# Transposing block-diagonal probabilities on VectorE, and output and gate rows of the samples by column groups, in a hybrid attention and DeltaNet decoder step

## The chip, the cores and the metric

The kernel runs on one core of one Trainium2 chip. The metric is the device time of one execution in microseconds.

## The reference

One inference step of a decoder layer with two parallel branches, for a prompt of 512 tokens and for 8 samples of 4 tokens each (32 rows). A conditioning vector `c` per sequence (1 for the prompt, 8 for the samples) gives shift, scale and gate. Branch A is softmax attention over three groups of heads with dilations 1, 4 and 16; branch B a gated DeltaNet. What the change touches is the gate, the attention's probabilities and the last lines, the output projection with its residual and LayerNorm:

```python
def layer_front(x, c, w_cond, b_cond, w_in):
    shift, scale, gate = jnp.split(jax.nn.silu(c) @ w_cond + b_cond, 3, axis=-1)
    h = x * (1 + scale[:, None]) + shift[:, None]
    return gate, split_columns(h @ w_in)
...
def dilated_attend(q, k_slab, v_slab, pos0, dilation, bias_hj):
    ...
    logits = jnp.einsum('bqhd,bqjhd->bqhj', q, k_sel, preferred_element_type=jnp.float32) * (A_HEAD_DIM ** -0.5)
    logits = logits + bias_hj.astype(jnp.float32)
    logits = jnp.where(valid[:, None, :], logits, -jnp.inf)
    m = jnp.max(logits, axis=-1, keepdims=True)
    p = jnp.exp(logits - m)
    s = jnp.sum(p, axis=-1, keepdims=True)
    out = jnp.einsum('bqhj,bqjhd->bqhd', p / s, v_sel.astype(jnp.float32))
...
def layer_back(x, gate, o_a, za, o_b, zb, ga, gb, b_norm_w, w_branch_a, w_branch_b, w_out, ln_g, ln_b):
    ...
    merged = jax.nn.sigmoid(ga) * (ya @ w_branch_a) + jax.nn.sigmoid(gb) * (yb @ w_branch_b)
    r = (ALPHA * x + gate[:, None] * (merged @ w_out)).astype(jnp.float32)
    mu = jnp.mean(r, axis=-1, keepdims=True)
    var = jnp.mean(jnp.square(r - mu), axis=-1, keepdims=True)
    return ((r - mu) * lax.rsqrt(var + LN_EPS)).astype(dtype) * ln_g + ln_b
```

`ALPHA` is 2 to the power 1/4; D_MODEL is 1024. Beside the two outputs `y`, the step returns updated key and value caches and states, which are mostly copied.

## The kernel before

The whole step is one program. Python functions record operations on symbolic tiles (`Recorder.add`), each with a rank; `Recorder.schedule` then places all of them with a list scheduler that has its own table of costs, and `emit` writes them in that order. So nearly all instructions carry one line, L723, and tiles have to be told apart by name. An operation counts as ready when the operations that it needs are done plus a margin, `Recorder.margin`: 0.1 for a compute operation on another engine, 0.5 for a transfer. Within an engine the order is then fixed, and each engine runs its instructions strictly in that order. All transfers are issued on SP's queue, the copies of the caches (`out_kv_s<-in_cache`) among them, which the scheduler puts between the others.

Products with the large weights are done in three products each (high part by high part, low by high, high by low) on `F32R` tiles. These are the stream of column jobs: 544 columns (512 prompt tokens and 32 sample rows) in two halves of 272, tiles `pp<-hhi,hi` and the like. Weights come in as `wt`, ScalarE makes the high part `hi`, VectorE the low part `lo`. PSUM has 2 banks for `pp`, 2 for `pd`, 3 for `pg`, 1 for `pb`. While the stream runs, threads of smaller work are mixed in: attention of the prompt, attention of the samples, DeltaNet.

**Attention of the prompt** (`prompt_attention`) runs over 4 head pairs `j`, 4 query blocks `i` of 128 queries, 2 heads `hh`. `scores` makes a tile `P` of 128 queries by 512 keys: 256 for group 0 (the block before and the own one), 128 for group 1 and 128 for group 2. In group 2 the dilation is 16, keys and queries are sorted by their residue, and `bias_indices` lets a query see only keys with `a == k // 32`, so that outside four 32x32 diagonal blocks all entries are zero after the exponential. TensorE transposes the quarters of `P` (3 of them for `i` = 0, else 4) into a bank `pg`; ScalarE (for `hh` = 0) or VectorE (`hh` = 1) copies them into `PT`, and `PT` is the moving operand of the products with `vrow`.

**Gate rows** (`gate_rows`, rank 1, between the column jobs of branch A): `gate` is `silu(c) @ w_cond + b_cond` for 9 rows (prompt and 8 samples). For each half `n` of 512 columns, 8 products `pd<-wc,cs` in two groups of 4; each of the four writes its own 32 partitions of a bank (`tile_position`), so the sum over the four partition groups is still to be taken. ScalarE copies the bank to `Y`, and two products with constant selections add up the groups and spread the rows: one makes `gp`, the prompt's row on 128 partitions, the other `gs`, the sample rows on 64. VectorE adds them to the bias, which was loaded into `gp` and `gs` beforehand.

**Output rows.** `merge_after` makes high and low parts `mhi`, `mlo` of `merged` and, for the 32 sample rows, a tile `ms` of 64 columns (high and low side by side). `load_out` loads `w_out` in four pieces of 512 KB per half (`wo`, through the 3 buffers of `wraw`) and makes `wo0h`, `wo0l`, `wo1h`, `wo1l`. The last loop goes over `ORDER`, pairs of a half `n` and a token tile `tt` (4 is the samples): 24 products of 512 columns for a token tile; 16 of 64 columns over 512 for the samples. VectorE multiplies by the gate, which frees the bank, adds the scaled input `xr`, takes the statistics, and after the second half normalizes; then `y` is written.

## Time and profile before

| what | us |
|---|---|
| median of three runs | 901.5 (900.58 to 903.18) |
| the profiled execution, its own time | 900.46 |
| its span in the profile | 898.7 |
| TensorE matmuls busy | 877.9 (98%) |
| VectorE busy | 718.9 (80%) |
| ScalarE busy | 428.7 (48%) |
| transfers, mean busy share of the 16 engines | 79% (the main queue) |

The profile shows one execution. Starts are counted from the span's start. A matmul's shown duration is longer than the time for which it keeps TensorE from the next one, since matmuls are pipelined: what one costs is read from the distance of starts. A fp32 product appears as two matmuls, a product of `F32R` tiles as one, a transpose as one.

### The profile page before, as it was taken

What the parts mean: (1) busy time and instruction counts of PE and PEld (TensorE: products, weight loads), DVE (VectorE), ACT (ScalarE), POOL (GpSimd) and SP (SyncE); (2) the same over time, 40 slices, a digit from 0 to 9 for tenths busy, and PEclk for the clock granted to TensorE, in tenths of its full rate; (3) what the DMA queues carried; (4) which work ended last, traced back from release to release, by engine and by line L of the source; (5) the groups of instructions that cost most, each with busy time, mean ns of one, the idle gap of its engine ahead of it and who ended that gap; (6) DMA issues with size and microseconds to landing.
All of it is one profiled execution on the core that took longest, in us unless ns stands there. A gap on an engine that the chain in (4) does not pass through costs nothing.

```text
span 898.7 us, 20349 instructions
## 1 busy us (share of the span) xinstructions
PE 877.9 (98%) x7864; PEld 827.9 (92%) x7864; DVE 718.9 (80%) x1580; ACT 428.7 (48%) x1054; POOL 51.0 (6%) x115
## 2 busy tenths in 40 slices
PE   8999999999999999999999999999999999999996
PEld 7889998999999998997999998999999999998676
DVE  3576657677669999987999997577989989958677
ACT  3474645676445776344666444544432222234321
POOL 0110010001000020000020000011010000000000
PEclk9999999999999999999999999999999999999999
DMA  9867787366787888897788887499799999989842
GB/s 367 317 177 217 219 237 245 141 175 228 229 254 253 246 259 283 260 310 249 265 270 278 245 290 229 135 324 391 229 336 347 348 407 410 356 259 334 305 130 100
DMA packets 104197, 239.39 MB, mean 266 GB/s; under 512 B 31955, under 2 KB 58589, under 8 KB 100389
## 3 DMA queue, kind: packets, MB, share of 16 engines
q1 hardware_dynamic: 103956, 238.08, 78.8%
q8 instruction: 62, 1.02, 0.4%
q14 instruction: 35, 0.28, 0.1%
q10 hardware_dynamic: 144, 0.01, 0.0%
HBM read 221.48 MB, written 104.26 MB: 362 GB/s over the span
## 4 chain that ended last, share of the span: by engine, by line
PE 84%; DMA 5%; DVE 4%; ACT 4%; issue 1%; POOL 1%; SPq 1%; DVEq 0%; POOLq 0%; ACTq 0%
PE pp L723 64%; PE pg L723 10%; PE pd L723 7%; PE pb L723 3%; DMA wt<-in_w_in 1%; DMA xT<-in_xT 1%; DMA wf<-in_w_first 1%; ACT L723 1%; DVE acc L723 1%; DMA wm<-in_w_mod 1%; DVE lo L723 1%; POOL ext L723 1%; ACT QKd L723 1%; SPq L723 1%; ACT hi L723 1%
## 5 line engine op out<-in xcount | busy, mean ns | idle before, releaser
L723 PE MATMUL pp<-hhi,hi 128*128 128x272 f32 x1360 | 399.0, 293 | 3.5 <-ACT ext L723 1.2
L723 PE MATMUL pp<-hlo,hi 128*128 128x272 f32 x1360 | 399.6, 294 | 0.0
L723 PE MATMUL pp<-hhi,lo 128*128 128x272 f32 x1360 | 398.7, 293 | 0.0
L723 PEld LDWEIGHTS pp<-hhi,hi 128*128 128x128 f32 x1360 | 256.5, 189 | 5.7 <-issue 2.4
L723 PEld LDWEIGHTS pp<-hhi,lo 128*128 128x128 f32 x1360 | 256.2, 188 | 2.4 <-issue 1.8
L723 PEld LDWEIGHTS pp<-hlo,hi 128*128 128x128 f32 x1360 | 256.6, 189 | 1.9 <-issue 1.2
L723 ACT ACTIVATE hi<-wt 128x1024 fp32r<-128x1024 f32 (+1 forms) x101 | 103.7, 1027 | 151.5 <-PE pp L723 123.0
L723 DVE TENSOR_TENSOR lo<-wt,hi 128x1024 fp32r<-128x1024 f32 (+1 forms) x101 | 118.7, 1175 | 37.3 <-ACT hi L723 36.5
L723 DVE SCALAR_TENSOR_TENSOR acc<-ext,cw,acc 128x568 f32<-128x568 f32 x72 | 57.1, 800 | 8.0 <-ACT acc L723 7.7
L723 ACT ACTIVATE P<-P,st 128x256 f32<-128x256 f32 (+1 forms) x64 | 31.2, 488 | 29.5 <-DVE st L723 29.2
L723 DVE TENSOR_TENSOR slab<-slab 128x512 f32<-128x512 f32 (+1 forms) x66 | 42.9, 664 | 2.6 <-DMA slab<-qd 2.6
L723 DVE TENSOR_REDUCE slab<-slab 128x8 f32<-128x512 f32 (+2 forms) x66 | 42.8, 658 | 0.2
L723 PE MATMUL pp<-ybl,hi 128*128 128x272 f32 x128 | 37.1, 290 | 0.0
L723 PE MATMUL pp<-ybh,hi 128*128 128x272 f32 x128 | 36.9, 288 | 0.0
L723 PE MATMUL pp<-ybh,lo 128*128 128x272 f32 x128 | 36.8, 288 | 0.0
L723 ACT ACTIVATE zt<-pp 128x272 f32<-128x272 f32 x48 | 18.7, 389 | 37.7 <-PE pp L723 34.4
L723 ACT ACTIVATE q<-pp 64x272 f32<-64x272 f32 (+1 forms) x48 | 26.3, 549 | 18.8 <-PE pp L723 18.2
L723 ACT ACT_TABLE_LOAD x26 | 33.4, 1283 | 1.6 <-PEq L2348 1.2
L723 PE MATMUL pg<-k,q 128*128 128x128 f32 (+1 forms) x192 | 33.6, 308 | 0.0
L723 PEld LDWEIGHTS pg<-k,q 128*128 128x128 f32 x192 | 27.3, 191 | 2.6 <-issue 1.3
L723 DVE CUSTOM_DVE_ANT_0 P<-pg,bias 128x256 f32<-128x256 f32 (+1 forms) x64 | 23.4, 399 | 5.7 <-PE pg L723 5.5
L723 DVE TENSOR_TENSOR tmp<-Ls,Tb 32x15 f32<-32x15 f32 (+7 forms) x120 | 23.1, 193 | 5.2 <-DMA Ls<-dblk 1.7
(399 smaller groups left out, 1601.9 us busy)
## 6 DMA issues: line engine op xcount, KB each, us to landing
out_kv_s<-in_cache SPq DMA_DIRECT2D x144, 512.0 KB
wt<-in_w_in SPq DMA_DIRECT2D x85, 512.0 KB
out_kv_s<-in_cache SPq DMA_DIRECT2D x24, 496.0 KB
wm<-in_w_mod SPq DMA_DIRECT2D x8, 1024.0 KB
slab<-in_ks SPq DMA_DIRECT2D x32, 256.0 KB
slab<-in_vs SPq DMA_DIRECT2D x32, 256.0 KB
kv<-in_ks SPq DMA_DIRECT2D x16, 512.0 KB
kv<-in_vs SPq DMA_DIRECT2D x16, 512.0 KB
```

What stands on the lines that cost most here:

```text
L723: getattr(real[x.engine], x.name)(*map(arg, x.args), **{k: arg(v) for k, v in x.kw.items()})
```

## The change

- **Attention.** TensorE transposes the first three quarters of `P` only. The last one (group 2) is transposed by VectorE, from `P` straight into `PT`, as `STREAM_TRANSPOSE`, which transposes within 32x32 blocks. The copies out of `pg` are narrower by 128 columns.
- **Gate rows.** All 8 products of a half stand in one group. The selection takes 9 columns and runs twice over 256 columns, each on its own column group, so that the 9 rows lie in 4 column blocks (`b4`), where the bias is added. These are written to DRAM (`dg`), and `gp` and `gs` are read back from there; `gs` now has 4 column blocks of 256 on 4 x 32 partitions.
- **Sample rows** (`sample_rows`, at (1, 4); (0, 4) is gone). In fp32, with `ms` of 32 columns as the stationary operand: for each of 8 `k`, four products over 256 columns of `w_out`, each on its own column group. The raw pieces of `w_out` are its moving operands: for the second half those that `load_out` has loaded (the fourth into a buffer of its own), for the first half four loaded again (`wr`). Means over 1024 columns are taken over the four groups by two products with a constant (`QUARTER`).
- **Margins.** `nudge` gives each operation a margin of its own out of a random generator: over all operations 0.35 to 0.65 for transfers and 0.06 to 0.14 for the others, and in 25 stretches of the recording, other values of one of three kinds (a transfer's margin, 0.3 to 0.9; the other margin, 0 to 0.2; TensorE's patience before it changes the tile form).

```diff
--- before.py
+++ after.py
-ORDER = ((0, 4), (0, 0), (0, 1), (0, 2), (1, 0), (1, 4), (1, 1), (1, 2), (0, 3), (1, 3))
+NUDGES = (
+    (0, 9912, 1047), (572, 972, 696727), (6242, 7442, 352100), (4626, 5026, 884219), (8230, 9430, 221759),
...
+ORDER = ((0, 0), (0, 1), (0, 2), (1, 0), (1, 4), (1, 1), (1, 2), (0, 3), (1, 3))
...
+QUARTER = (np.arange(128)[:, None] % 32 == np.arange(128)[None, :] % 32).astype(np.float32) / 4
...
+    def nudge(self):
+        for lo, hi, seed in NUDGES:
+            rng, kind = np.random.default_rng(seed), seed % 3 if lo else 3
+            for op in self.ops[lo:hi]:
+                x = rng.uniform()
+                if kind in (0, 3):
+                    op.load_margin = 0.3 + 0.6 * x if kind == 0 else 0.35 + 0.3 * x
+                if kind in (1, 3):
+                    op.own_margin = 0.2 * x if kind == 1 else 0.06 + 0.08 * rng.uniform()
+                if kind == 2 and op.engine == "pe":
+                    op.hold = self.HOLD * (0.5 + 1.2 * x)
+
     def schedule(self):
         ops = self.ops
         tag, lines = {}, {}
+        self.nudge()
...
-        return 0.1 if p.transfer is None else 0.5
+        return getattr(op, "own_margin", 0.1) if p.transfer is None else getattr(op, "load_margin", 0.5)
...
-                    for c in range(c0_, 4):
+                    for c in range(c0_, 3):
                         pe.transpose(pt[:, 128 * c:128 * c + 128], Ps[hh][:, 128 * c:128 * c + 128], ident)
                     PT = ap.tile([128, 4, 128], F32, name="PT", bufs=2)
                     eng = ve.tensor_copy if hh else (lambda o, x: se.activation(o, x, AF.Copy))
-                    eng(PT[:, c0_:], cols128(pt)[:, c0_:])
+                    eng(PT[:, c0_:3], cols128(pt)[:, c0_:3])
+                    ve.transpose(PT[:, 3], Ps[hh][:, 384:512])
...
-        sp.dma_start(gp, b.to_broadcast([128, D]))
-        sp.dma_start(gs, b.to_broadcast([64, D]))
+        b4 = al.tile([128, 256], F32, name="b4")
+        for q in range(4):
+            sp.dma_start(b4[32 * q:32 * q + 9], b[:, 256 * q:256 * q + 256].to_broadcast([9, 256]))
         ps = [pd(), pd()]
         yield 4.0
         for n in range(2):
             w = slice(512 * n, 512 * n + 512)
 
-            for k0 in range(0, KT, 4):
-                wc = []
-                for k in (k0, k0 + 2):
-                    wc.append(wcp.tile([128, 2, 512], F32, name="wc"))
-                    sp.dma_start(wc[-1], cond_rows(k, 2)[:, :, w])
-                with rec.together():
-                    take(cond_product(2, lambda part: ((k0 + k, n, wc[k // 2][:, k % 2]) for k in range(4)), ps), 99)
-                yield 2.0
+            wc = []
+            for k in range(0, KT, 2):
+                wc.append(wcp.tile([128, 2, 512], F32, name="wc"))
+                sp.dma_start(wc[-1], cond_rows(k, 2)[:, :, w])
+            with rec.together():
+                take(cond_product(2, lambda part: ((k, n, wc[k // 2][:, k % 2]) for k in range(KT)), ps), 99)
+            yield 2.0
             Y = zp.tile([128, 512], F32, name="Y", tag="rbo")
             se.activation(Y, ps[n], AF.Copy)
             yield 1.8
-            for t, r, sel in ((gp, 128, C("selc")[:, 0:1].to_broadcast([128, 128])), (gs, 64, C("selg"))):
-                p = pg()
-                pe.matmul(p[0:r], sel, Y, start=True, stop=True)
-                ve.tensor_add(t[:, w], t[:, w], p[0:r])
+            p = pg()
+            with rec.together():
+                for u in range(2):
+                    q = 2 * n + u
+                    pe.matmul(p[32 * q:32 * q + 9, 0:256], C("selc"), Y[:, 256 * u:256 * u + 256], start=True, stop=True,
+                              tile_position=(0, 32 * q))
+            for q in (2 * n, 2 * n + 1):
+                v = slice(32 * q, 32 * q + 9)
+                ve.tensor_add(b4[v], b4[v], p[v, 0:256])
+                sp.dma_start(dg[:, 256 * q:256 * q + 256], b4[v])
+        sp.dma_start(gp, dg[0:1].to_broadcast([128, D]))
+        for q in range(4):
+            sp.dma_start(gs[32 * q:32 * q + 32], dg[1:9, None, 256 * q:256 * q + 256].to_broadcast([8, 4, 256]))
...
-    ms = al.tile([128, 8, 64], F32R, name="ms")
+    ms = al.tile([128, 8, NS], F32, name="ms")
     gp = al.tile([128, D], F32, name="gp")
-    gs = al.tile([64, D], F32, name="gs")
+    gs = al.tile([128, 256], F32, name="gs")
...
+    def raw_load(n, k, raw):
+        sp.dma_start(raw, io["w_out"][k * 128:k * 128 + 256, 512 * n:512 * n + 512].rearrange("(a p) c -> p a c", a=2))
+        raw_out[n, k] = raw
+        return raw
+
     def load_out(n):
 
         for k in range(0, KT, 2):
-            raw = wraw.tile([128, 2, 512], F32, name="wo", tag="wraw")
-            sp.dma_start(raw, io["w_out"][k * 128:k * 128 + 256, 512 * n:512 * n + 512].rearrange("(a p) c -> p a c", a=2))
+            raw = (o1.tile([128, 2, 512], F32, name="wr", bufs=3) if n and k == 6 else
+                   wraw.tile([128, 2, 512], F32, name="wo", tag="wraw"))
+            raw_load(n, k, raw)
...
+    dg = dram.tile([9, D], F32, name="dg")
     wctx = ExitStack()
-    wcp = pool(wctx, "wcp", 3, "right")
+    wcp = pool(wctx, "wcp", 4, "right")
...
-            se.activation(ms[:, m, 0:32], t[:, SEQ:], AF.Copy)
-            ve.tensor_sub(ms[:, m, 32:64], t[:, SEQ:], ms[:, m, 0:32].bitcast(F32))
+            se.activation(ms[:, m], t[:, SEQ:], AF.Copy)
...
-    lo4 = o1.tile([32, 512], F32, name="lo4")
+    for k in range(0, KT, 2):
+        raw_load(0, k, wsp.tile([128, 2, 512], F32, name="wr", tag="hi") if k < 4 else
+                 o1.tile([128, 2, 512], F32, name="wr", bufs=3))
+    ln4 = o1.tile([128, 2 * 256 + 128], F32, name="ln4")
+    sp.dma_start(ln4, io["ln_s"])
+    x4 = o1.tile([128, 256], F32, name="x4")
+    sp.dma_start(x4, io["x_s"])
...
+    def sample_rows():
+        po = pd()
+        with rec.together():
             for k in range(KT):
-                for i, (a, b) in enumerate(parts(k)):
-                    pe.matmul(po, a[:, 128 * tt:128 * tt + 128], wo[n][b][:, k, w],
-                              start=(k == 0 and i == 0), stop=(k == 7 and i == 2))
-            return po
-
-        for k in range(KT):
-            for b in range(2):
-                pe.matmul(po[0:64], ms[:, k], wo[n][b][:, k, w], start=(k == 0 and b == 0), stop=(k == 7 and b == 1))
-        return po[0:64]
+                for q in range(4):
+                    wr = raw_out[q // 2, k - k % 2][:, k % 2, q % 2 * 256:q % 2 * 256 + 256]
+                    pe.matmul(po[32 * q:32 * q + 32, 0:256], ms[:, k], wr, start=(k == 0), stop=(k == 7),
+                              tile_position=(0, 32 * q))
+        se.activation(x4, x4, AF.Copy, scale=ALPHA)
+        y = o1.tile([128, 256], F32, name="y4")
+        ve.scalar_tensor_tensor(y, po[:, 0:256], 0.5, gs, op0=OP.mult, op1=OP.mult)
+        ve.tensor_add(y, y, x4)
+        bn4 = o1.tile([128, 6], F32, name="bn4")
+        ve.bn_stats(bn4, y)
+        mv = o1.tile([128, 6], F32, name="mv4")
+        ve.bn_aggr(mv[:, 0:2], bn4)
+        quarter = ln4[:, 512:640]
+        pm = pd()
+        pe.matmul(pm[:, 0:1], quarter, mv[:, 0:1], start=True, stop=True)
+        ve.tensor_copy(mv[:, 2:3], pm[:, 0:1])
+        ve.tensor_sub(mv[:, 3:4], mv[:, 0:1], mv[:, 2:3])
+        ve.scalar_tensor_tensor(mv[:, 4:5], mv[:, 3:4], mv[:, 3:4], mv[:, 1:2], op0=OP.mult, op1=OP.add)
+        pv = pd()
+        pe.matmul(pv[:, 0:1], quarter, mv[:, 4:5], start=True, stop=True)
+        se.activation(mv[:, 5:6], pv[:, 0:1], AF.Sqrt, bias=eps5[:, 0:1])
+        ve.scalar_tensor_tensor(y, y, mv[:, 2:3], ln4[:, 0:256], op0=OP.subtract, op1=OP.mult)
+        ve.reciprocal(mv[:, 5:6], mv[:, 5:6])
+        ve.scalar_tensor_tensor(y, y, mv[:, 5:6], ln4[:, 256:512], op0=OP.mult, op1=OP.add)
+        for q in range(4):
+            sp.dma_start(io["y_s"][:, 256 * q:256 * q + 256], y[32 * q:32 * q + 32])
...
+        if tt == 4:
+            sample_rows()
+        else:
+            pr_, gate = slice(0, 128), gp
...
-                if tt == 4:
-                    ve.scalar_tensor_tensor(lo4, po[32:64], 0.5, gate[32:64, w], op0=OP.mult, op1=OP.mult)
-                    ve.tensor_add(xr[pr_], xr[pr_], lo4)
```

The order that the scheduler makes of it differs in nearly every row. Three places:

First, TensorE between the output tile (1,0) and (1,1). `wo1h`, `wo1l` are parts of the second half of `w_out`, `mhi`, `mlo` those of `merged`, `ms` the sample rows, `wr`, `wo` raw pieces of `w_out`. Before:

```order
L723 MATMUL pp_11381<-wo1h_11269,mhi_11243 128x512
L723 MATMUL pp_11381<-wo1l_11295,mhi_11243 128x512
L723 MATMUL pp_11381<-wo1h_11269,mlo_11250 128x512
L723 MATMUL pp_11419<-wo1h_11269,ms_10840 64x512
L723 MATMUL pp_11419<-wo1l_11295,ms_10840 64x512
```

Now:

```order
L745 MATMUL pp_11356<-wo1l_11300,mhi_11257 128x512
L745 MATMUL pp_11356<-wo1h_11281,mlo_11263 128x512
L745 MATMUL pd_11385<-wr_11189,ms_10832 32x256 x2
L745 MATMUL pd_11385<-wo_11182,ms_10832 32x256 x2
L745 MATMUL pd_11385<-wr_11189,ms_10832 32x256 x2
L745 MATMUL pd_11385<-wo_11182,ms_10832 32x256 x2
L745 MATMUL pd_11385<-wr_11248,ms_10832 32x256 x2
L745 MATMUL pd_11385<-wo_11225,ms_10832 32x256 x2
```

Where 16 products of 64 columns over 512 stood (and 16 of the first half elsewhere), 32 of 32 columns over 256 now stand in 8 groups of four.

Second, SP's queue where the gates' and the output weights' transfers stand. Before, the bias comes straight into `gp` and `gs`, some 20 rows ahead of the loads `wo`:

```order
L723 DMA out_kv2_s<-in_cache2 16x8192
L723 DMA wc_10663<-in_w_cond 128x2x512
L723 DMA gp_10670<-in_b_cond 128x1024
L723 DMA gs_10677<-in_b_cond 64x1024
L723 DMA wc_10696<-in_w_cond 128x2x512
L723 DMA wc_10716<-in_w_cond 128x2x512
L723 DMA wt_10722<-in_w_ga 128x512
```

Now the second writes of `dg` and the reads of `gs` and `gp` stand between the loads `wo` of the first half:

```order
L745 DMA wo_11075<-in_w_out 128x2x512
L745 DMA dg_10924<-b4_10667 9x256 x2
L745 DMA out_kv2_s<-in_cache2 16x8192
L745 DMA gs_11016<-dg_10924 32x1x256
L745 DMA wo_11152<-in_w_out 128x2x512
L745 DMA gp_11157<-dg_10924 128x1024
L745 DMA wo_11165<-in_w_out 128x2x512
L745 DMA gs_11016<-dg_10924 32x1x256
L745 DMA out_kv2_s<-in_cache2 16x8192
L745 DMA wo_11182<-in_w_out 128x2x512
L745 DMA wr_11189<-in_w_out 128x2x512
```

Transfers that wait for a VectorE result and for a write to land now stand ahead of the loads for the last stage.

Third, VectorE at a query block of the first head pair. `P` are the probabilities, here with the bias added (ISA), `st` their row maxima. Before:

```order
L723 ISA P_2003,st_1942<-pg_1990,bias_622 128x256
L723 ISA st_1942 128x1
L723 COPY NB_2021<-pg_2005 128x4x32
L723 TENSOR_TENSOR lo_2029<-wt_1738,hi_1987 128x1024
L723 COPY PT_2050<-pg_2024 128x512
L723 SCALAR_TENSOR_TENSOR acc_2054<-ext_1023,cw_612,acc_2054 128x568
L723 STREAM_TRANSPOSE Xc_2065<-Tc_1591 128x256
```

Now:

```order
L745 ISA P_1980,st_1926<-pg_1973,bias_624 128x256
L745 ISA st_1926 128x1
L745 STREAM_TRANSPOSE PT_2016<-P_1988 128x128
L745 STREAM_TRANSPOSE Xc_2023<-Tc_1571 128x256
L745 STREAM_TRANSPOSE PT_2028<-P_1980 128x128
L745 COPY PT_2016<-pg_2013 128x384
L745 COPY W_2051<-pd_1644 128x8x16
```

Two transposes of 128x128 stand beside a copy of 384 columns in place of one of 512.

## Rows read from the trace of the kernel before

**Rows 1.** The page: the span, and busy time and share of each engine.
```profile
span 898.7 us, 20349 instructions
...
PE 877.9 (98%) x7864; PEld 827.9 (92%) x7864; DVE 718.9 (80%) x1580; ACT 428.7 (48%) x1054; POOL 51.0 (6%) x115
```

**Rows 2.** What TensorE waited for: us in total, times, longest; first and last.
```profile
PE pd L723 <- issue: 1.7, 1, 1.7
...
PE pg L723 <- ACT Sa L723: 0.2, 1, 0.2
```

**Rows 3.** Timeline of TensorE in attention: start us, us, engine, instruction, count.
```profile
142.49 0.38 PE L723 MATMUL pg<-cst,P 128*128 128x128 f32 x2
142.63 0.37 PE L723 MATMUL pp<-hhi,lo 128*128 128x272 f32 x1
...
163.96 0.60 PE L723 MATMUL pg<-cst,P 128*128 128x128 f32 x4
164.31 0.37 PE L723 MATMUL pp<-hhi,hi 128*128 128x272 f32 x1
```

**Rows 4.** The same timeline at the gate rows' products.
```profile
814.55 1.06 PE L723 MATMUL pd<-wc,cs 128*32 128x512 f32 x8
815.54 0.39 PE L723 MATMUL pp<-yah,lo 128*128 128x272 f32 x1
...
816.40 0.29 PE L723 MATMUL pp<-yah,lo 128*128 128x272 f32 x1
...
817.61 1.07 PE L723 MATMUL pg<-Y,cst 128*64 128x512 f32 x2
818.61 0.39 PE L723 MATMUL pp<-yal,hi 128*128 128x272 f32 x1
```

**Rows 5.** The same timeline, sample rows of the first half.
```profile
837.36 0.39 PE L723 MATMUL pp<-wo0h,ms 128*64 128x512 f32 x1
837.59 0.39 PE L723 MATMUL pp<-wo0l,ms 128*64 128x512 f32 x1
```

**Rows 6.** The same timeline, quads of 32 columns: two at the start, one later.
```profile
15.46 1.07 PE L723 MATMUL pd<-wm,cs 128*32 128x256 f32 x16
16.46 0.39 PE L723 MATMUL pp<-hhi,whi 128*128 128x272 f32 x1
...
726.38 0.29 PE L723 MATMUL pp<-ybh,hi 128*128 128x272 f32 x1
726.60 0.64 PE L723 MATMUL pg<-kv,Qz 128*32 128x256 f32 x8
727.17 0.39 PE L723 MATMUL pp<-ybl,hi 128*128 128x272 f32 x1
727.40 0.29 PE L723 MATMUL pp<-ybh,lo 128*128 128x272 f32 x1
```

**Rows 7.** Groups of VectorE by shape: xcount, busy us, mean ns, idle before.
```profile
L723 DVE COPY W<-pd 32x256 f32<-32x256 f32 x8 | 3.4, 424 | 3.6 <-PE pd L723 3.4
...
L723 DVE COPY S<-pd 128x128 f32<-128x128 f32 x8 | 2.3, 285 | 3.1 <-PE pd L723 3.1
...
L723 DVE STREAM_TRANSPOSE Xc<-Tc 128x256 f32<-128x256 f32 x4 | 1.8, 438 | 0.0
```

**Rows 8.** Busy time by stretch: PE, PEld, DVE, ACT, POOL, clock, DMA share, GB/s.
```profile
270.00:303.00 33.00, 33.00 (x449) 30.46 (x448) 32.47 (x89) 20.77 (x70) 1.18 (x2) 1.00 0.76 244
402.00:436.00 34.00, 32.83 (x481) 28.24 (x480) 27.62 (x84) 19.81 (x64) 2.33 (x4) 1.00 0.73 248
800.00:842.00 42.00, 41.47 (x289) 33.01 (x287) 29.19 (x54) 16.22 (x30) 0.00 (x0) 1.00 0.90 311
```

**Rows 9.** Timeline of SP's queue and of VectorE around `dw`.
```profile
581.86 0.31 SPq L723 DMA_DIRECT2D dw<-pack  x1
...
585.35 1.12 SPq L723 DMA_DIRECT2D wv<-dw  x2
...
593.48 0.68 DVE L723 TENSOR_TENSOR ya<-ya,NB 128x512 f32<-128x512 f32 x1
```

More of the change, by code (lines that the diff above doesn't have):

```diff
@@ L42 @@
 S0B = 7
[L43 removed]
+NUDGES = (
[6 rows of a table added]
+)
+ORDER = ((0, 0), (0, 1), (0, 2), (1, 0), (1, 4), (1, 1), (1, 2), (0, 3), (1, 3))
 def column_tiles():
@@ L2229, in product_out @@
-        return po[0:64]
+        for k in range(KT):
+            for i, (a, b) in enumerate(parts(k)):
+                pe.matmul(po, a[:, 128 * tt:128 * tt + 128], wo[n][b][:, k, w],
+                          start=(k == 0 and i == 0), stop=(k == 7 and i == 2))
+        return po
+    def sample_rows():
+        po = pd()
+        with rec.together():
+            for k in range(KT):
+                for q in range(4):
[24 more added lines that the diff above has]
+            sp.dma_start(io["y_s"][:, 256 * q:256 * q + 256], y[32 * q:32 * q + 32])
```

19 lines of the change are left out of this document (9 added, 10 removed), and 5 rows, old and new, of the table NUDGES.

## The prediction

> **What bounds the kernel now.** I read the busy table first: the span is 898.7 us and TensorE's matmul row is busy for 877.9 us of it, VectorE for 718.9 [rows 1]. A busy TensorE row can hide waits, since ends of matmuls are modelled, so I read two more views. The list of what TensorE waited for has 14 lines, the longest 1.7 us in total and the last 0.2, and they add up to 12.8 us [rows 2]. In the timeline a 272-column product of the main stream starts every 0.125 us where nothing disturbs it, and it does so almost everywhere. TensorE executes its instructions in order, and a background stream of column products fills it while other work is awaited. So the rule for this kernel: **a microsecond of TensorE instructions that disappears is a microsecond of time**, unless another engine, or the transfers, can't keep up with the earlier start. [...]
>
> **Part 1, transposes (attention, `prompt_attention`).** Of each probability tile of 128x512, the last quarter (head group 3, where a query sees only keys of its own residue) is zero outside its four 32x32 diagonal blocks, so a transpose within blocks is enough. There are 4 head pairs x 4 query blocks x 2 heads = 32 such quarters. TensorE loses 32 transposes. A run of two holds it for 142.63 - 142.49 = 0.14 us, a run of four for 164.31 - 163.96 = 0.35 [rows 3]; so one more in a run costs (0.35 - 0.14)/2 = 0.105 us, and 32 are **3.4 us**. The last quarter is one of three or four in a run, so no run disappears and no switch of form is saved.
> VectorE gains 32 transposes of 128x128. The trace has none of that size: a block transpose of 128x256 takes 0.438 us, a copy out of PSUM with 256 columns 0.424, one with 128 columns 0.285 [rows 7]. The copy is my lower bound, the larger transpose the upper; I take 0.30, since at 256 columns the transpose lies 0.014 above the copy. That is 9.6 us (9.1 to 14.0). The 16 evacuations on VectorE narrow by 128 columns, 0.139 us each by the same two copies: -2.2. Net +7.4 us on VectorE (6.9 to 11.8), of which a quarter falls on each head pair. Beside pair 3 VectorE has room, being busy 27.6 of 34 us. Beside pair 2 it is busy 32.5 of 33 us, but TensorE is busy for all 33 there [rows 8]. I cost it at nothing on the path: the stream's products cover it, and the order puts the two transposes ahead of the narrower copy, where before the whole copy stood. Without that cover it is the first rival below.
> [...] The rows show that a TensorE transpose costs 0.105 us of the engine that sets the time [rows 3], while VectorE's costs three times as much on an engine with slack. [...]
>
> **Part 2, gate rows.** The products with `wc` come in two groups of eight in place of four of four. One group of four with 512 columns holds TensorE 815.54 - 814.55 = 0.99 us [rows 4]. To what this costs for entering and leaving the 32-column form: entering 726.60 - 726.38 - 0.125 = 0.095, leaving 727.40 - 727.17 - 0.125 = 0.105 [rows 6]. The second four of a group cost no form change and, from the 256-column groups, twice (1.00 - 0.57) = 0.86: two quads of 256 columns take 16.46 - 15.46 = 1.00 and one takes 727.17 - 726.60 = 0.57. So each pair of groups goes from 2 x (0.99 + 0.20) = 2.38 to 0.99 + 0.86 + 0.20 = 2.05, and the two pairs save 0.7 us. The selection products: between 816.40 and 818.61 stand both of them and two stream products, 2.21 - 0.25 = 1.96, and with leaving 2.07 [rows 4]. Now two products of 9 columns on two column groups, at 256 columns: at most what a full quad costs, 0.57 + 0.20 = 0.77. Twice 1.30 = 2.6. **Part 2 is 3.3 us** (2.9 to 3.6, the upper end if half a quad is a little cheaper).
> What is added: the gates now go through DRAM. Four small writes of `dg`, then `gp` and four pieces of `gs` are read back on SP's queue. Behind the first of these reads, which waits for its write, the loads `wo` stand, and behind those `wr`; for the `wo` wait the products of the last stage. The nearest round trip in the trace is `dw`: written at 581.86, read from 585.35, its last reader on VectorE runs at 593.48 at the earliest [rows 9], so 3.5 us to the read and 11.6 in all. In the order of the changed kernel, 80 stream products and 24 of `wo0` (0.23 each, [rows 5]) stand between the second selection product and the end of the first output tile: 10.0 + 5.5 = 15.5 us. And a second PSUM bank takes the next tile, another 5.5. So `gp` has 15.5 to 21 us for 11.6 plus about 1; I cost it at nothing.
>
> **Part 3, sample rows.** 32 products of 64 columns over 512, one every 837.59 - 837.36 = 0.23 us [rows 5], go: 7.4 us. In their place stand 8 quads of 32 columns over 256 in fp32, back to back: 0.57 + 7 x 0.43 + 0.20 = 3.8 us [rows 6]. Two products with one column each are added to average over the four column groups, 128x128 in fp32; two passes at 0.105 and a change of mode, so 0.25 each, 0.5 in all (0.2 to 2, if they wait: the mean has to come from VectorE, and TensorE has 8 products of 0.23, 1.8 us, until then against four VectorE steps, three of them with 256 columns at some 0.42 [rows 7]). **Part 3 is 7.4 - 3.8 - 0.5 = 3.1 us.** On VectorE twice five operations of 512 columns become three of 256, which helps it in a busy tail.
> What is added beside it: `w_out`'s first half is loaded again, 2.1 MB, and the constants `ln4` and `x4`, 0.46 MB. In the order they come after the last stage's pool opens and ahead of the first `xr`: with `lng`, `lnb` and that `xr` some 3.3 MB, at 311 GB/s [rows 8] 10.6 us. The first `xr` is wanted when (1,0) ends, 77 products of 0.23 or 17.7 us after the pool opens. So 7 us are left for the landing and for what is queued before; I cost it at nothing.
> [...]
>
> **Part 4, margins.** The table of random margins changes no instruction, only where the planner puts each. What it costs or brings can come from TensorE's waits alone, 12.8 us in all [rows 2]; by the order ScalarE also gets 6 more table loads (26 before, 32 now), on an engine with slack. I take zero and a third of 12.8, 4.3 us, either way for the range.
>
> **Sum.** 3.4 + 3.3 + 3.1 = 9.8 us. The profiled execution took 900.46 us with a span of 898.7, some 1.0 below the median of the three runs, 901.5. Off the profiled run that is 890.7, off the median **891.7 us**, 1.1% less.
>
> **Rivals.**
> (a) VectorE takes the gain of part 1. For it: 32.5 of 33 us busy beside pair 2. Price: that pair's share, 8 x 0.30 - 4 x 0.139 = 1.8 us; at the upper bound and with pair 3 too 2 x (8 x 0.438 - 0.56) = 5.9. Time 893.5 to 897.6; I take 895.5. Against: TensorE shows no wait there.
> (b) The transfers can't follow. For it: the 16 engines are busy 0.90 of the stretch from 800 to 842 [rows 8], so the 6.7 us of parts 1 and 2 come back as waits for `wt` and `wo` before the last stage. What is left is part 3: 898.4. Against: much of the load there are cache copies that the planner places freely, and the order has six of them behind the first `xr`, where there were four.
> (c) Slower than before: the tail waits for `xr`. VectorE is in order, and the addition of the first `xr` stands ahead of the evacuation that frees the next PSUM bank and of the mean that the one-column product waits for. From 17.7 us after the pool's opening on, each us that `xr` is late is a us of the end; it takes 12.5 us more to be slower by over 0.3%, so a landing 30 us after the opening, 109 GB/s in place of 311. That is 904.2 and more; I take 905. Against: the rate.
> (d) The 64 weight loads of the sample rows are not hidden. At most all of the 0.43 us again for each of the 8 quads, 3.4 us: 895.1. Against: the 0.43 already has the loads in it.
> (e) The new order's waits shrink or grow by 4.3 us: 887.4 or 896.0.
>
> **How the numbers follow.** Forecast 0.58; (a) 0.11; (b) 0.10, of which half is within 0.3% (above 898.8); (c) 0.04; (d) 0.03; (e) 0.07 shorter and 0.07 longer, 0.04 of the latter so long together with (a) that it ends within 0.3%. A difference under 0.3%, 2.7 us, is what a measurement of this kernel can't tell from none. Faster: 0.58 + 0.11 + 0.05 + 0.03 + 0.07 + 0.03 = 0.87, of which I move 0.02 to the middle for what I have not thought of; within 0.3%: 0.05 + 0.04 + 0.02 = 0.11; slower 0.04. The range goes from 887.0, (e) shorter, to 898.4, (b).
>
> **What will show it.** TensorE's instructions: runs of transposes with one fewer; the 64 instructions of the quads in about 3.6 us; the selection products at 0.6 us. VectorE's transposes at 0.30 us. TensorE's list of waits near 12.8 us: if it is over 16, the step "at nothing" of part 1 or the margins failed; if a wait for `gp`, `wr` or `xr` stands in the last 55 us, that of part 2 or 3 did. The steps behind the last matmul are the same, and so should be the time from it to the end. If TensorE's busy time falls by 10 us and the span doesn't, the rule of the first paragraph is wrong.

## The result and the profile after the change

The changed kernel takes **888.3 us** (median of 6 runs, 886.9 to 890.4), the kernel before 902.3 us beside it (6 runs); the ratio is 0.984, with a 95% interval of 0.981 to 0.986. A second set of five runs, made later beside the variants below, gave 887.4 us and 0.983 (0.980 to 0.986). So 14 us are gone, where 9.8 were forecast. The time lies inside the predicted range (887.0 to 898.4) and close to its lower end.

The profile shown here is that of the second set, since the first profiled execution was the slowest of its six (its stream began 3 us late, behind a load of `wm` and 6.8 us, from 10.1 to 16.9, in which the granted clock was 0.50). First the page of the changed kernel, the span and the busy time of each engine, as in [rows 1]:

```profile
span 887.1 us, 20372 instructions
...
PE 869.4 (98%) x7868; PEld 824.0 (93%) x7868; DVE 715.0 (81%) x1599; ACT 431.7 (49%) x1059; POOL 40.3 (5%) x115
```

TensorE is busy 8.5 us less and the span is 11.6 us shorter than in the profiled execution of before. What TensorE waited for (us in total, times, longest; the first two lines and the last of 12, which sum to 9.6 us, where [rows 2] had 14 and 12.8):

```profile
PE pp L745 <- ACT cx L745: 2.5, 1, 2.5
PE pd L745 <- ACT Y L745: 1.1, 1, 1.1
...
PE pb L745 <- ACT vr L745: 0.2, 1, 0.2
```

VectorE's groups by shape (count, busy us, mean ns), the operations that [rows 7] only bounded:

```profile
L745 DVE STREAM_TRANSPOSE PT<-P 128x128 f32<-128x128 f32 x32 | 9.4, 299 | 0.8 <-ACT P L745 0.6
...
L745 DVE COPY PT<-pg 128x384 f32<-128x384 f32 x12 | 6.5, 544 | 0.5 <-PE pg L745 0.4
```

The 128x128 transpose takes 0.299 us; the prediction had taken 0.30. The copy of 384 columns takes 0.142 us less than the one of 512 in the kernel before, where 0.139 was forecast:

```profile
L723 DVE COPY PT<-pg 128x512 f32<-128x512 f32 x12 | 8.2, 686 | 2.9 <-PE pg L723 2.8
```

TensorE's timeline at the gate rows (start, us, instruction, count), to be read against [rows 4]:

```profile
815.15 1.92 PE L745 MATMUL pd<-wc,cs 128*32 128x512 f32 x16
817.01 0.39 PE L745 MATMUL pp<-yal,hi 128*128 128x272 f32 x1
...
819.08 0.61 PE L745 MATMUL pg<-Y,cst 128*9 128x256 f32 x4
819.62 0.39 PE L745 MATMUL pp<-yal,hi 128*128 128x272 f32 x1
```

Eight `wc` products hold TensorE 817.01 - 815.15 = 1.86 us (1.85 without the form change by the forecast), the selection 819.62 - 819.08 = 0.54, so with the same 0.2 for entering and leaving 0.74 (0.77 was the bound). And the sample rows, against [rows 5]:

```profile
852.45 0.41 PE L745 MATMUL pd<-wr,ms 128*32 128x256 f32 x2
...
855.06 1.05 PE L745 MATMUL pd<-wr,ms 128*32 128x256 f32 x16
856.04 0.50 PE L745 MATMUL pp<-wo1h,mhi 128*128 128x512 f32 x1
...
858.00 0.28 PE L745 MATMUL pd<-mv,ln 128*128 128x1 f32 x2
858.14 0.48 PE L745 MATMUL pp<-wo1h,mlo 128*128 128x512 f32 x1
858.47 0.40 PE L745 MATMUL pp<-wo1h,mhi 128*128 128x512 f32 x1
```

The eight quads take 856.04 - 852.45 = 3.6 us, and a one-column product costs 858.47 - 858.00 - 0.23 = 0.24: both as forecast (3.8 with 0.2 for the form change, and 0.25). So the local prices came out as forecast. The stretch of the gate rows and the stream's last products, as the last of [rows 8]:

```profile
795.00:836.00 41.00, 40.94 (x297) 34.88 (x296) 27.77 (x47) 16.45 (x30) 0.00 (x0) 1.00 0.91 317
```

The transfers are busy 0.91 of it, and TensorE 40.94 of 41 us. That makes the 4 us on top the question, and with it whether the other 10 are really those of the edits.

### The profile page after: what moved, and what is told of

The parts are those of the page before. It is cut to its first block, busy times and chain, and to the rows that moved or that the text cites. A ratio compares the mean times of both kernels' runs of the same rounds, so it can differ in the third digit from the quotient of the medians.

```text
span 888.6 us, 20372 instructions
## 1 busy us (share of the span) xinstructions
PE 871.0 (98%) x7868; PEld 825.9 (93%) x7868; DVE 714.8 (80%) x1599; ACT 431.8 (49%) x1059; POOL 40.7 (5%) x115
## 4 chain that ended last, share of the span: by engine, by line
PE 87%; DVE 4%; ACT 4%; DMA 2%; issue 1%; SPq 1%; POOL 1%; DVEq 0%; ACTq 0%; POOLq 0%
PE pp L745 65%; PE pg L745 9%; PE pd L745 9%; PE pb L745 3%; ACT L745 1%; DMA wm<-in_w_mod 1%; DMA wv<-dw 1%; DVE acc L745 1%; SPq L745 1%; DVE ya L745 1%; PE warm L745 0%; DVE NB L745 0%; ACT ext L745 0%; DVE XF L745 0%; POOL q L745 0%
## 5 line engine op out<-in xcount | busy, mean ns | idle before, releaser
L745 ACT ACTIVATE q<-pp 64x272 f32<-64x272 f32 (+1 forms) x48 | 26.2, 545 | 17.4 <-PE pp L745 16.9
```

The source lines that it names most:

```text
L745: getattr(real[x.engine], x.name)(*map(arg, x.args), **{k: arg(v) for k, v in x.kw.items()})
```

## The experiments

**The parts, without the table of margins.** Each of these four kernels lets the scheduler make its own order. The first takes the table away and keeps the three edits:

```diff
-NUDGES = ((0, 9912, 1047), (572, 972, 696727), ...)
+NUDGES = ()
```

> The changed kernel with an empty table of margins; every margin is as before (0.1 and 0.5). Theory A, by which the three edits are worth what the prediction summed (9.8 us) and the rest of the 14 us comes from the order that the margins make: 892 us, 0.989 of before, and some 4 us slower than the changed kernel. Theory B, by which the edits themselves are worth 14 us and were under-sized: 888 us, 0.984. Theory C, by which the margins are worth nothing on average and a new order alone scatters by some us: between the two, with no side.

Measured: **905.9 us** (12 runs, 901.6 to 908.2; ratio to before 1.003, 1.0004 to 1.005). None of the three theories had this: without the table the three edits gain nothing, and the table is worth 18 us. I then ran each part alone. The transposes, put into the kernel before:

```diff
-                    for c in range(c0_, 4):
+                    for c in range(c0_, 3):
...
-                    eng(PT[:, c0_:], cols128(pt)[:, c0_:])
+                    eng(PT[:, c0_:3], cols128(pt)[:, c0_:3])
+                    ve.transpose(PT[:, 3], Ps[hh][:, 384:512])
```

> The kernel before with the last quarter of each probability tile transposed by VectorE, nothing else. Prediction's step: 32 x 0.105 = 3.4 us off, 898.5 us. Rival (a), VectorE takes it back: 1.5 us or less off. Theory B (under-sized): 6 us or more off, 896. VectorE's transpose of 128x128: 0.30 us by the step, 0.285 to 0.438 by its bounds.

Measured: 912.1 us (6 runs), ratio 1.010 (1.008 to 1.012), so 9.7 us slower. The gates through DRAM alone (the `wc` groups and the sample rows as before, so `gs` keeps its 64 rows):

```diff
-                pe.matmul(p[0:r], sel, Y, start=True, stop=True)
...
+                    pe.matmul(p[32 * q:32 * q + 9, 0:256], C("selc"), Y[:, 256 * u:256 * u + 256], start=True, stop=True,
+                              tile_position=(0, 32 * q))
...
+                sp.dma_start(dg[:, 256 * q:256 * q + 256], b4[v])
+        sp.dma_start(gp, dg[0:1].to_broadcast([128, D]))
```

> The kernel before with the gate rows' selection on two column groups and the way through DRAM, but with the condition products still in two groups of four for each half (four buffers do not fit here), the sample rows as before. Prediction's step: 2.6 us off, 899.5 us, and no wait for gp or gs in TensorE's list. Rival: the round trip through DRAM shows as a wait before the last stage, 2 to 10 us, and the time is that of before or above.

Measured: 904.2 us (12 runs), ratio 1.002 (0.9996 to 1.004). And the sample rows by column groups alone (the gates as before, but the sample gates spread by two products on column groups):

```diff
+                    pe.matmul(po[32 * q:32 * q + 32, 0:256], ms[:, k], wr, start=(k == 0), stop=(k == 7),
+                              tile_position=(0, 32 * q))
```

> The kernel before with the sample rows by column groups alone. Transposes and the condition products as before; the prompt's gate row by the old product, the sample gates by two products on two column groups, since the layout needs it. Prediction's step: 7.4 - 3.8 - 0.5 = 3.1 us off, and up to 0.4 for the smaller selection: 898.7 us. Rival (d), weight loads not hidden: the 64 instructions take some 7 us in place of 3.6 and nothing is left. Rival (c), the tail waits for the inputs: 902 us or more.

Measured: 905.3 us (12 runs), ratio 1.002 (1.0003 to 1.004); its quads take the same 3.6 us.

Where does the gain go? I added up, for each product of TensorE, the time from its start to the next product's start, and compared the edits without margins with the kernel before (us, from the two traces; a wait counts with the product ahead of it, a form change with the products around it):

```text
saved in place   transposes 3.8; sample rows 7.4 - 3.6 - 0.3 = 3.5; selection and wc 2.9 + 0.3 - 1.1 = 2.1   sum 9.4
lost elsewhere   DeltaNet chain (pb<-cst,KQ 2.7, pd<-z 2.6, pd<-S,KQ 2.6, pd<-vn 2.0)                        9.9
                 pg<-PT,vrow 3.0; warm (filler products) 2.6; all other products together 0.4                6.0
```

So the edits save in place about what the prediction said, and 16 us come back elsewhere, most of them in stretches that no edit touches: the list scheduler, given other operations, made another order everywhere. Two places show what such an order costs. In the first, TensorE of the edits without margins around 315 us (the bracket is the idle time and what ended it):

```profile
312.44 0.49 PE L738 MATMUL pd<-vn,kr 128*128 128x128 f32 x2 [0.92 <-ACT vn L738]
...
313.89 0.83 PE L738 MATMUL warm<-ones 128*128 128x128 f32 x6
...
315.00 0.61 PE L738 MATMUL warm<-ones 128*128 128x128 f32 x4
...
316.05 0.83 PE L738 MATMUL warm<-ones 128*128 128x128 f32 x6
...
317.77 0.39 PE L738 MATMUL warm<-ones 128*128 128x128 f32 x2
...
320.49 0.40 PE L738 MATMUL pp<-hhi,hi 128*128 128x272 f32 x1 [1.22 <-ACT ext L738]
```

The stream of column products, which should cover the DeltaNet chain, stands still, since its next bank waits for ScalarE's `ext`; the chain's own waits lie bare, and the scheduler fills with `warm` products that compute nothing. In the changed kernel the trace has no wait and no `warm` from 300 to 318 us. The second place is at 560 us, where nearly all of the 3.0 us of `pg<-PT,vrow` are one wait; the transposes alone have the same place with a wait of 3.24 us:

```profile
559.12 0.69 PE L738 MATMUL pd<-Tc,NTs 32*32 32x32 f32 x32
559.75 0.87 PE L738 MATMUL pg<-PT,vrow 128*64 128x128 f32 x11
563.33 0.80 PE L738 MATMUL pg<-PT,vrow 128*64 128x128 f32 x5 [2.71 <-issue]
```

Busy time by stretch (columns as in [rows 8]) of the same kernel, before and behind this wait:

```profile
545.00:560.00 15.00, 15.00 (x237) 13.95 (x238) 11.86 (x39) 6.99 (x23) 1.00 (x3) 1.00 0.85 257
560.00:575.00 15.00, 12.29 (x144) 10.60 (x141) 7.80 (x27) 5.10 (x17) 0.00 (x0) 0.77 0.17 51
```

In the middle of a group TensorE waits 2.7 us for nothing that a semaphore shows, and behind it the granted clock is 0.77 on the mean of 15 us. The one level below 1.00 in the trace of the kernel before and in that of the first profiled execution of the changed kernel is 0.50 (in the latter from 337.8 to 341.2 us, where a 272-column product starts every 0.23 us and not every 0.125); at that level it would be 2 x 0.23 x 15 = 6.9 us of the 15. What it waited for, I take up below.

The gates alone show one more thing, the wait that the prediction had costed at nothing:

```profile
847.12 0.39 PE L723 MATMUL pp<-wo0h,mlo 128*128 128x512 f32 x1
850.37 0.50 PE L723 MATMUL pp<-wo0h,mhi 128*128 128x512 f32 x1 [2.87 <-DVE r L723]
```

VectorE there sat idle 3.9 us for the landing of `gp<-dg`, whose transfer had been issued at 842.0. In the changed kernel it is issued at 824.0, and its first reader runs at 838.2; there it waits for TensorE, not for the gates. The first reader in the gates alone and in the changed kernel:

```profile
849.63 0.69 DVE L723 SCALAR_TENSOR_TENSOR r<-pp,gp 128x512 f32<-128x512 f32 x1 [3.91 <-DMA gp<-dg]
```

```profile
838.15 0.69 DVE L745 SCALAR_TENSOR_TENSOR r<-pp,gp 128x512 f32<-128x512 f32 x1 [1.13 <-PE pp L745]
```

So the round trip is free or costs 2.9 us by where the order puts it.

**The transposes with the order held.** To tell an edit from its order, I let the scheduler order the kernel before, and made the edit when the instructions were written out, so that everything else stays where it stood:

```diff
+        if x.name == "transpose" and names[:2] == ["pg", "P"]:
+            self.probs[id(x.outs[0].base)] = x.ins[0].base
+            if int(x.ins[0].ix[0, 0]) == 384:
+                return
+        elif names[:2] == ["PT", "pg"]:
...
+            yield "ve", "transpose", (PT[:, 3], P[:, 384:512]), {}
...
+            yield x.engine, x.name, (out[:, 0:k], a[:, 0:k]) + tuple(x.args[2:]), x.kw
```

> The kernel before, with its order held: the 32 transposes of the last quarters leave TensorE, VectorE gets a 128x128 transpose right ahead of each narrower copy, and every other instruction of every engine stays where it stood (in the run with the transposes alone the scheduler had made a new order, and it was 9.7 us slower). Theory C, the edit is worth what the prediction said and the loss of 9.7 us was the new order's: 32 x 0.105 = 3.4 us less than before, 899.0 us, TensorE's waits as in before. Rival D, VectorE takes the gain back because ScalarE's and VectorE's copies and the products behind them come later: 902 to 908, with waits for PT or P in the list of TensorE.

Measured: 902.2 us (12 runs) against 903.9 for the kernel before in this set, ratio 0.9987 (0.997 to 1.0006). So 9.7 us slower became 1.2 us faster, not to be told from nothing: the loss was the order's, as theory C says, but only a part of the 3.4 us arrives. In the profiled execution the transposes themselves take 3.6 us less from start to start, and yet its last matmul starts 1.7 us later than in the profile of before. The largest single part of what comes back stands here:

```profile
556.02 0.43 PE L742 MATMUL pd<-Tc,NTs 32*32 32x32 f32 x14
558.20 0.69 PE L742 MATMUL pd<-Tc,NTs 32*32 32x32 f32 x18 [1.74 <-issue]
```

Again a wait in which nothing is awaited, and again the clock goes behind it (0.83 on the mean from 555 to 565 us; 1.00 from 5 to 896 us in the kernel before). The kernel before has a wait near this place too, a shorter one:

```profile
554.43 0.30 PE L723 MATMUL pg<-cst,qs 128*64 128x128 f32 x1
555.81 0.27 PE L723 MATMUL pg<-cst,qs 128*64 128x128 f32 x1 [1.08 <-DVE Tc L723]
```

From 553 to 561 us the order-held run loses 2.0 us on the kernel before. The rest comes back in small pieces, some of them in front of results of VectorE. From TensorE's list of waits, the kernel before and the order-held run:

```profile
PE pb L723 <- DVE QKd L723: 1.0, 2, 0.9
```

```profile
PE pb L742 <- DVE QKd L742: 1.7, 2, 1.5
...
PE pg L742 <- DVE NB L742: 0.5, 1, 0.5
...
PE pd L742 <- DVE XF L742: 0.3, 1, 0.3
```

The reverse, in the changed kernel with its order held: the transposes go back to TensorE.

```diff
+        if x.name == "transpose" and names[:2] == ["PT", "P"]:
+            return
...
+        if x.name == "transpose" and names[:2] == ["pg", "P"] and int(x.ins[0].ix[0, 0]) == 256:
+            yield "pe", "transpose", (full(x.outs[0].base)[:, 384:512], full(x.ins[0].base)[:, 384:512], x.args[2]), {}
```

> The changed kernel, with its order held: the 32 transposes go back to TensorE, each right behind the one of the third quarter, the copies are full again, VectorE's 32 transposes are gone, nothing else moves. Theory C: 3.4 us slower than the changed kernel, 891.7 us. Rival D: within 1 us of it, 888 to 889, since VectorE had taken the gain back; rival E, the changed kernel's order only fits its own durations and breaks up when 0.1 us is added in 32 places: 895 or more.

Measured: 888.9 us (5 runs), 1.5 us above the changed kernel itself in the same set:

> The changed kernel itself, beside its variants on the same chip: 888.3 us as before. Its profiled execution was the slowest of six (890.4 us); this one should have the start of the stream as the kernel before has it, at some 47 us in place of 50.

887.4 us (5 runs), its stream beginning at 47.1 us, as expected. Both ways the medians give the transposes 1 to 2 us of 3.6, and neither difference is clear of the scatter of the runs. Rival D (VectorE takes the gain back) is not excluded. The waits of the first of the two sum to 14.5 us where those of the kernel before sum to 12.8; none is a wait for `PT` or `P`, as rival D had it, but those for VectorE's `QKd`, `NB` and `XF` are 1.5 us longer.

**Other margins.** The same rows and stretches with other random numbers, twice (every seed plus 3, plus 300), and the table of the change on the kernel before, whose operations have other numbers:

```diff
-    (0, 9912, 1047), (572, 972, 696727), ...
+    (0, 9912, 1050), (572, 972, 696730), ...
```

> The changed kernel with the same 26 rows of its table of margins, same stretches and kinds, but every seed larger by 3, so other random numbers. Theory F, the table is one lucky order among many, and what a random order gives scatters around the three edits without margins (905.9 us): 900 to 912. Rival G, margins that differ from operation to operation are better as such, whatever the numbers: 887 to 891.

Measured: 898.9 us (10 runs, 898.1 to 900.8).

> The changed kernel with every seed of the table larger by 300: a third draw of random margins in the same stretches. Theory F, each order is a draw, and the table of the change is a chosen one: anywhere from 895 to 910, TensorE's list of waits longer than the 9.5 us of the changed kernel by about what the time is longer. Rival, random margins as such are worth some 7 us against none (905.9 without, 898.9 with the first other draw): 896 to 901.

Measured: 906.2 us (10 runs).

> The kernel before, none of its three edits, but with the table of margins of the change, so with a new order. Theory F: a draw like the others, since the table was chosen for the changed kernel's recording: 898 to 912 (before: 902.4). Rival, the margins as such bring the gain and the edits 3: 885 to 893.

Measured: 905.1 us (10 runs), ratio to before 1.001 (0.999 to 1.003).

So margins as such bring nothing that one can count on (7 us less and 0.3 more than no margins; on the kernel before, 2.0 more); the numbers of this table do, and not with the recording of before. The longer waits that theory F foretold for the third draw are there, but make up only 7.1 of its 18.2 us. Four orders of the same three edits, with TensorE's list of waits summed and its `warm` products counted (the first median is that of both sets):

```text
                      us      waits   warm   span profiled
table of the change   888.0    9.6     48     887.1
seeds + 3             898.9   15.9     64     898.9
no margins            905.9   18.4     66     905.1
seeds + 300           906.2   16.7     76     904.1
```

The order accounts for 11 to 18 us. Of the 18.0 us between the spans of the first and the third, 18.4 - 9.6 = 8.8 are waits and 2.6 `warm` products. Of the other 6.6, up to 0.23 x 15 = 3.5 are the lower clock behind 560 us; each of the two traces has a shorter stretch of it elsewhere (0.95 on the mean from 270 to 303 us in the first, 0.91 from 440 to 460 us in the third; at 0.50 that is 3.3 and 3.6 us), and these cancel.

**What "issue" is.** The profile writes `issue` where an engine waited for nothing that it shows. I counted TensorE's instructions in each trace (matmuls, weight loads and the few others) and looked where the waits of more than 0.7 us stand in which TensorE awaited nothing. There are 22 such gaps, from start to start, in 14 traces, and all stand 193 or 194 above a multiple of 256:

```text
before 154.4, 418.3; after 420.3; no margins 155.5, 560.3; transposes alone 154.9, 559.7; gates alone 154.4, 420.0; ...
place modulo 256: 194, 194; 193; 193, 193; 193, 193; 194, 194; ...
```

The waits for a semaphore stand anywhere (in the gates alone at 5, 141, 255, 154, 28, ...). And the page has a queue that it calls `instruction` (packets, MB, share): of the changed kernel, and of the next two kernels,

```profile
q8 instruction: 62, 1.02, 0.5%
```

```profile
q8 instruction: 63, 1.03, 0.5%
```

```profile
q8 instruction: 64, 1.05, 0.5%
```

62 packets for 15,891 counted instructions (7868 matmuls, 7868 weight loads, 155 others) are 256 each, and every packet has 16,384 bytes in the trace. So I take the place at which TensorE waits for the one where a new packet of its own code begins.

The trace also has the time at which each packet was moved. Each of the 22 gaps ends 1.25 to 1.62 us after the end of such a transfer, which took 0.9 to 1.2 us and had begun 2.3 to 6.1 us after TensorE passed the place 256 instructions earlier. Two waits at the place 193 that the list puts down to `DVE Tc` (the 1.08 us at 556 us in the kernel before, and 0.75 us in the gates alone) end in the same way, 1.3 and 1.45 us after a packet. For the wait of 2.71 us in the kernel without margins, TensorE passes that earlier place at 555.3 us. The queues that moved anything from there to 561.0 us, and the code queue from 561.0 to 562.0 us (packets, MB, share):

```profile
q1 hardware_dynamic: 487, 1.64, 87.6%
```

```profile
q8 instruction: 1, 0.02, 6.0%
```

The packet moves from 561.01 to 561.97 us, and TensorE goes on at 563.33. To move the place, I issued a group of short products several times, three times in the changed kernel:

```diff
+        if x.engine == "pe" and names == ["pd", "NTs", "Tc"] and len(self.repeat) < 32:
+            self.repeat.append((x.engine, x.name, x.args, x.kw))
+            if len(self.repeat) == 32:
+                for _ in range(2):
+                    yield from self.repeat
```

> The changed kernel, with its order held, but the first group of 32 small products pd<-Tc,NTs (at some 117 us, 32x32 form, 16 columns) is issued three times in place of once: 64 matmuls more, with the same result. They cost 2 x 0.3 = 0.6 us, and all of TensorE's later instructions stand 128 places later in its stream (a matmul and its weight load are two). Theory H: TensorE's waits in which it waits for nothing are waits for its own code. In all traces so far each of those above 0.7 us stands at the same place, 193 or 194 above a multiple of 256 instructions, and the page has 62 packets of 16 KB of instructions, 256 of 64 bytes each. Shifted by 128, one such multiple falls so that its 256 instructions run in 2.8 us near 414 us (in the unshifted order the shortest is 3.9 us, near 271, and it waits 1.0 there): a new wait of 1.5 to 4 us near 414, again at 193 or 194, the one near 271 gone, and the total 890 to 893. Rival: those waits belong to the products at which they stand: 0.6 us more, 888.0 to 888.9, with the wait near 271 still there.

Measured: 894.0 us (6 runs, 890.3 to 896.8), 6 us above the changed kernel. The place that I had named was wrong, for a mistake of mine: each of these products is two matmuls and two loads in the trace, so that 64 of them are 256 instructions and not 128. All later code stood one whole packet later, at the same place within it, and this run shifts nothing. (The repeated products also stand at 146 us and not at 117, since half of the 32 were ordered there.) What it shows is a wait of 2.73 us where the next packet begins, behind a burst of 256 more short instructions and in products that had none:

```profile
148.15 0.29 PE L757 MATMUL pd<-W,Xc 32*32 32x16 f32 x10
151.17 0.63 PE L757 MATMUL pd<-W,Xc 32*32 32x16 f32 x54 [2.73 <-issue]
```

The second run repeats the group three more times in the kernel without margins, 384 instructions, so that the later code does stand half a packet later:

> The three edits without margins (905.9 us), with their order held, but the first group of 32 products pd<-Tc,NTs is issued four times in place of once: 96 matmuls more, 0.9 us, and all later instructions stand 192 places later. [...] Total 902 to 905. [...]

Measured: 910.5 us (6 runs), 4.6 us slower than without the repeats. By theory H the wait of 2.7 us at `pg<-PT,vrow` had to go, and it has gone: the products at which it stood now run through in one piece (5 us on, at 571 us, a wait of 0.98 us stands at the place 194):

```profile
566.27 0.69 PE L750 MATMUL pd<-Tc,NTs 32*32 32x32 f32 x32
566.89 1.09 PE L750 MATMUL pg<-PT,vrow 128*64 128x128 f32 x16
```

and the mean clock from 566 to 572 us is 1.00. Between 528 and 594 us this run made up 4.3 us on the one that it was made from. But the burst itself made the longest wait of all,

```profile
151.19 1.39 PE L750 MATMUL pd<-Tc,NTs 32*32 32x16 f32 x144
157.09 1.26 PE L750 MATMUL pd<-Tc,NTs 32*32 32x16 f32 x80 [4.51 <-issue]
```

and from its start on this stretch, in the columns of [rows 8]:

```profile
152.00:170.00 18.00, 13.49 (x349) 12.28 (x338) 6.54 (x19) 3.16 (x10) 0.78 (x2) 0.72 0.19 77
```

With a mean clock of 0.72 there, the products at 186 us came 7.6 us later than without the repeats. Theory H holds for what the wait is and where it stands, and its rival falls; both totals were missed, since I had not counted what the repeats themselves would do.

This also says what a held order doesn't hold. With 32 transposes and their weight loads gone, TensorE's later instructions stand at other places in their packets: the kernel before has code waits of over 0.7 us at 156, 420 and 556 us, the order-held run at 156 and 558 us.

## Why the prediction came out as it did

- **The rule of the first paragraph** (a microsecond of TensorE instructions is a microsecond of time) is right only while the order stands, and then not in full. With the order held, 3.6 us of transposes were worth 1.2 us one way (by the interval from 2.8 us less to 0.5 more) and 1.5 the other; when the scheduler may order anew, the three edits, 9.4 us in place, were 3.4 us slower.
- **Part 1.** The price on VectorE (0.299 us against 0.30) was right. Moving the transposes there shows no loss: with the order held it is a gain of 1.2 us or nothing. The term of 3.4 us was right as TensorE's time and too large by about 2 us as time of the kernel. Rival (a) named the wrong place: beside pair 2 (270 to 303 us) the order-held run has no wait for VectorE (0.35 us for ScalarE's `vr`). Its gain comes back as a longer wait for code with a lower clock at 558 us (2.0 us), and in part as waits for VectorE's results elsewhere (1.5 us longer). How much VectorE takes back isn't settled by one profile.
- **Part 2.** Both local terms were right. "Nothing" for the round trip holds in the changed kernel (the read of `gp` is issued 14.2 us ahead of its first reader on VectorE) and not in general: 2.9 us in the gates alone.
- **Part 3.** Quads 3.6 us, one-column products 0.24, no wait for `wr`: right. Rival (d) falls with the quads: their 64 weight loads add nothing that can be seen here. A second quad of 512 columns takes 1.86 - 0.99 = 0.87 us and one of 256 columns (3.6 - 0.57) / 7 = 0.43, in proportion to the columns, though each has the same eight loads. The sum of the loads ahead of the first `xr` was wrong: they are 3.9 MB (`wr` 2.1, `ln4` and `x4` 0.46, `lng` and `lnb` 1.05, `xr` 0.26) and not 3.3, which leaves 5 us of the 7. It did no harm, and rival (c) falls too: TensorE has no wait above 0.2 us from 829 to 879 us, and from the start of the last matmul to the end it is 8.0 us, 7.8 before.
- **Rival (b)** falls: the transfers are as busy as forecast in the stage ahead of the output (0.91 in the stretch shown above), and TensorE's list has no wait for `wt` or `wo`.
- **Part 4 is the step that failed.** It took zero, and 4.3 us either way. I had taken the margins for a small disturbance of an order that the edits leave alone. They aren't small, and the edits don't leave it alone: without the table the new order takes back all that they save, and the time is 905.9 us where the sum said 891.7. Against other orders of the same edits the table is worth 11 to 18 us, two and a half to four times my bound, which I had drawn from the waits of *one* order, 12.8 us. Orders that the scheduler may make have up to 18.4 us of waits, fillers, and a lower clock on top.
- **The total** lies in the range by luck: the edits, forecast at 9.8 us, are slower by themselves, and the table, forecast at nothing, is worth more than the whole change. What the prediction had not joined is that this table's order lets the savings stand. Counted from start to start as above, the changed kernel saves 2.9 (transposes), 3.5 (sample rows) and 2.1 us (gates) in place, 8.5 in all, and its waits go from 12.8 to 9.6 us. 8.5 and 3.2 make 11.7; the profiled executions differ by 11.6 us, the medians by 14.1 and 16.5, in the main since the profiled execution of before is a fast one (900.46 us against medians of 902.3 and 903.9). The mean granted clock of the runs is 0.996 for both kernels, so it is no part of the difference. Against the order of before, rival (e), "shorter", was the right mechanism, and it had 0.07.

What stays open: which of the table's 26 rows matter, whether the gain of the table over the edits lies in a few places or in many (at least 3 us of its 18 are in neither waits, fillers nor the clock), and why the transfer of a code packet begins so much later in some places than in others. No run separates these.

## What to carry to other kernels

Where a scheduler makes the order, an edit's local price says what may be gained, and not what the run will show: hold the order and make the edit alone before you believe in a gain or a loss, since an edit here cost 9.7 us through the order and, with it held, made 1.2 us less, not to be told from nothing. Cost any table that changes an order by the spread of several orders, not by the waits of the one at hand. And look at the waits in which an engine awaits nothing: if they stand at equal distances in its instruction stream, as here, multiples of 256 instructions apart, suspect its code. Spreading the bursts of short instructions would be the thing to try; no run here did.

## What the runs showed of the hardware that I had not expected

TensorE's code came in packets of 16 KB, 256 instructions each (62 packets for the 15,891 instructions of the changed kernel). The stream's products of 272 columns used one up in some 16 us; stretches with bursts of 32x32 products used one up in 4.3 to 6.0 us (ahead of the waits at 154, 418 and 555 us in the kernel before, and of the one at 420 us in the changed kernel; with the repeats 288 instructions took 1.4 us), and then TensorE stood, for up to 4.5 us, at the place where I take the next packet to begin, until 1.25 to 1.62 us after a packet had been moved. Behind two of these waits (2.7 us and 4.5 us above) the granted clock was lower for a time: 0.77 on the mean of 15 us and 0.72 of 18, which at 0.50 is some 7 and 10 us. The length of a wait alone doesn't tell: in the gates alone the clock was 1.00 for 15 us behind a code wait of 2.60 us at 157 us, and 1.00 from 848 to 863 us around the wait of 2.87 us shown above (0.998 on the mean of that execution). The transfers run low behind the two waits (0.17 and 0.19 in the rows above), but low transfers and a low clock don't always go together: in the first profiled execution of the changed kernel they move 418 GB/s from 10.2 to 16.8 us at a clock of 0.50, and in the kernel before 3 GB/s from 160 to 165 us at 1.00. And a block transpose of 128x128 in fp32 on VectorE costs 0.299 us, 0.14 us less than one of 128x256.
